# Layer 0's second feed-forward shift and scale: from 32-column TensorE matmuls to VectorE reductions

## The chip, the cores and the metric

The kernel runs on one core of one Trainium2 chip. The metric is the device time of one execution in microseconds (us), the median over several runs; smaller is better. The core has five engines, each with its own in-order instruction stream: TensorE (PE in the profile, with its weight loads as PEld), VectorE (DVE), ScalarE (ACT), GpSimd (POOL) and SyncE (SP). SP and POOL issue the large transfers from device memory here.

## What is computed

A two-layer backbone over 256 latent tokens and 256 context tokens with 1024 features. Each layer has a SwiGLU feed-forward, a token mixing and a second SwiGLU, each behind an RMSNorm with a shift, a scale and a gate. These come from two condition vectors, one for the latent tokens and one for the context tokens, through one large matrix per layer. Cut to what matters:

```
mod_x = (silu(c) @ w_ada[l] + b_ada[l])[:, None, :]      # w_ada[l]: 1024 x 9216
mod_c = silu(c_ctx) @ w_ada[l] + b_ada[l]
sh1, sc1, g1, shm, scm, gm, sh2, sc2, g2 = split(mod_x, 9)
h = h + 0.5 * g1 * swiglu(modulate(rms_norm(h, norm_ffn1[l]), sh1, sc1), w_gate, w_up, w_down)
...                                                      # token mixing with shm, scm, gm
h = h + 0.5 * g2 * swiglu(modulate(rms_norm(h, norm_ffn2[l]), sh2, sc2), ...)
```

sh2 and sc2, the shift and scale of the second feed-forward, are 2 x 1024 numbers for each kind of token. They are first used after the token mixing.

## The kernel before

Activations lie feature-major: features on the 128 partitions, tokens in the free dimension. A weight tile of 128 x 1024 numbers (512 KB) is loaded by SP into a ring of three buffers ("raw") and split by `wload` (lines 124 to 126) into a high and a low float32r part: ACT copies the high part (L125), DVE subtracts to get the low part (L126). The pairs go into a ring of four buffers ("split"). A product is then three matmuls of 512 columns (`mm3`, lines 130 to 132: high x high, high x low, low x high).

The first feed-forward of layer 0 (`ffn`) is the stage that matters here. Its 22 hidden feature tiles are worked in parts of 6, 6, 6 and 4. A hidden tile `ft` takes 24 matmuls into a gate bank "pg" and 24 into an up bank "pu", two banks of each; ACT applies SiLU (L396), DVE multiplies (L397), ACT and DVE split the result into "G" (L398, L399). The first three hidden tiles are computed in an order written out by hand (`first_tiles`, banks "pf"). After a part, and one hidden tile of the next, the part's down projection runs: 8 output tiles of 18 matmuls each into a bank "pd", of which there are three in turn, and DVE adds each to the residual stream "H", one instruction for each kind of token (L259).

Between hidden tiles `run_jobs` calls a share of a list of jobs, so that by hidden tile 19 all are called. The tile scheduler then settles each engine's order; what follows names it where it counts. The jobs of layer 0 are:

- 32 jobs of `ada_dve` (lines 140 to 147), eight for each of g1, shm, scm and gm. A job loads 512 KB of the transposed matrix, 128 output features on the partitions, by POOL's queue into one of 8 buffers "araw" (L144), and takes two DVE instructions of 1024 elements (L147), one for each kind of token, that multiply by the condition vector "cb" and sum along the row.
- 16 jobs of `ada_pe_jobs` (lines 149 to 176) for sh2 and sc2. A job loads 512 KB of the untransposed matrix into one of the same 8 buffers (L158) and issues two matmuls (L160) with 32 columns of weights "csel" and 512 moving columns into the bank "adaps". At the end ACT copies the bank (L165), PE transposes it in four pieces (L168), DVE reduces those (L172) and adds bias and gain.

The two kinds are interleaved, two of the first for one of the second:

```
jobs += jd[:2] + jp[:1]
```

Of the kernel before, what the change touches and what calls it, by code (L numbers as in the profile page):

```python
# [25 lines left out]
BANKS = {"mm": 3, "s": 2, "t": 2, "o": 1}  # L26
PIECES = 4
NT0 = 6
# the order in which the steps of the first tiles are issued (see first_tiles)
START = (  # L30
# [4 lines left out]
)  # L35
# the order in which the steps of the two token mixings are issued (see mixer)
MIX = (
    (
# [10 lines left out]
    ),  # L49
)  # L50
# engines that scale the three tiles of probabilities (A: ScalarE, V: VectorE)
PN = ("AAV", "AVV")
EPS = 1e-6
NEG = -1e30
# [5 lines left out]
def hybrid_backbone(ctx: ExitStack, tc: tile.TileContext, I, out):  # L60
# [8 lines left out]
    def bank(tag, name):  # L69
        return psum.tile([128, 512], F32, tag=tag, name=name, bufs=BANKS[tag])  # L70
# [9 lines left out]
    stt = nc.vector.scalar_tensor_tensor  # L80
    ts_ = nc.vector.tensor_scalar

    # residual stream, feature-major: [feature, feature tile, token]
    H = up.tile([128, KT, TOK], F32, name="H")

    ident = const("ident", [128, 128], I["ident"], nc.scalar)
# [26 lines left out]
        qg8 = late["qg8"] = cp.tile([128, DEPTH], F32, name="qg8")  # L113
        nc.gpsimd.tensor_scalar(qg8, qkg[:, :, 0], 0.125, None, op0=ALU.mult)

# [1 line left out]
    def raw_load(src, n):  # L117
        raw = wp.tile([128, 1024], F32, tag="raw", name="raw", bufs=3)
        nc.sync.dma_start(raw[:, :n], src)
# [17 lines left out]
            mm3(ps, sp[:, 0, o:o + 128], sp[:, 1, o:o + 128], U[0][:, k0 + k, cols], U[1][:, k0 + k, cols],  # L137
                k == 0, k == nk - 1)

# [1 line left out]
    def ada_dve(l, ft, cb, ntok, pool):  # L141
        raw = pool.tile([128, 1024], F32, tag="araw", name="araw", bufs=ABUFS)
        with tc.issue_after(marks["pool"]):
# [1 line left out]
        scr = pool.tile([128, 1024], F32, tag="ascr", name="ascr", bufs=1)  # L145
        for t in range(ntok):
            stt(scr, raw, 1.0, cb[:, t, :], op0=ALU.mult, op1=ALU.mult, accum_out=ada[l][:, ft, t:t + 1])  # L147

    def ada_pe_jobs(src, l, ft0, nchunk, csel, pool, mods):
        box = {}  # L150

        def piece(c, j):
            if not box:
                box["ps"] = bank("o", "adaps")
            ps = box["ps"]
            raw = pool.tile([128, 1024], F32, tag="araw", name="araw", bufs=ABUFS)
            with tc.issue_after(marks["pool"]):
                nc.gpsimd.dma_start(raw, src[:, (c * 4 + j) * 1024:(c * 4 + j + 1) * 1024])  # L158
            for s in range(2):
                mm(ps[32 * j:32 * j + 32, :], csel[:, 2 * j + s, c, :], raw[:, s * 512:(s + 1) * 512],  # L160
                   start=(c == 0 and s == 0), stop=(c == nchunk - 1 and s == 1))

        def end():
            sb = pool.tile([128, 512], F32, tag="adasb2", name="adasb2", bufs=1)
            act(sb, box["ps"], AF.Copy)  # L165
            pt = bank("o", "adapt")
            for b in range(4):
                nc.tensor.transpose(pt[:, b * 128:(b + 1) * 128], sb[:, b * 128:(b + 1) * 128], ident)  # L168
            v = pt.rearrange("p (b j r) -> p b r j", b=4, j=4)
            for c in range(nchunk):  # L170
                f = ft0 + 4 * c
                nc.vector.tensor_reduce(ada[l][:, f:f + 4, :], v[:, :, 2 * c:2 * c + 2, :], axis=AX.X, op=ALU.add)  # L172
            for m in mods:
                ada_fin(l, m)

        return [lambda c=c, j=j: piece(c, j) for c in range(nchunk) for j in range(4)] + [end]

    def ada_fin(l, m, ntok=2, ds=slice(0, KT)):
        i = MODS.index(m)
# [16 lines left out]
        i = MODS.index(m)  # L196
        return ada[l][:, i * KT:(i + 1) * KT, :]

# [1 line left out]
    accs, adds = {}, {}  # L200

    def norm_sq(half, d, eng=nc.gpsimd, pool=None):
        # the sum of squares: tiles 0 .. 6 into one accumulator, tile 7 on its own
        cols = (LAT, CT)[half]
        if d == 0:
            t = npl.tile([128, 256], F32, tag="acc", name="acc", bufs=2)
            accs[half] = [t, None]
        else:
            if pool:
                t = pool.tile([128, 2, TOK], F32R, tag="G", name="sq0", bufs=10)[:, 0, :256].bitcast(F32)  # L210
            else:
                t = npl.tile([128, 256], F32, tag="sq", name="sq", bufs=2)
        act(t, H[:, d, cols], AF.Square)
        if d == KT - 1:
            accs[half][1] = t
        prev = adds.pop(half, None)
        if prev is not None:
            (nc.vector if d >= DV else eng).tensor_tensor(accs[half][0], accs[half][0], prev, ALU.add)
        if 0 < d < KT - 1:
            adds[half] = t  # L220
# [63 lines left out]
        return after  # L284

    def first_tiles(pool, csel, U, src):
        # adaLN's first shift and scale come in feature pieces; NT0 output tiles take each piece as it arrives
        # r, s: 1 / rms of a half of the tokens; a, b, c: a piece of the vectors; w, x: a tile's weights in two parts;
        # u, v: the two parts of a normalised feature tile; m: a feature tile's share of an output tile
        pss, sps, rb, ada_ps, ada_pt, rstd, tmp = [], [], [], {}, {}, {}, {}  # L290

        def r(h):
# [6 lines left out]
            next(rstd[h], None)  # L299

        def a(p, i):
            # a quarter of the rows of w_ada for shift (c = 0) or scale (c = 1), by four column groups of the array
            if i == 0:
                ada_ps[p] = bank("mm", "adaps")
            c, b = divmod(i, 2)
            raw = pool.tile([128, 4, 256], F32, tag="araw", name="araw", bufs=ABUFS)
            nc.sync.dma_start(raw, I["w_ada0"][:, p, c, b])
            for j in range(4):
                mm(ada_ps[p][32 * j:32 * j + 32, :256], csel[:, 2 * j + b, c, :], raw[:, j, :], start=(i == 0),
                   stop=(i == 3))  # L310
# [60 lines left out]
                steps[o[0]](*map(int, o[1:]))  # L371
        return pss

# [1 line left out]
    def ffn(l, w, halves, pool, U, jobs, after, start=None):  # L375
        both = len(halves) == 2
        N = 256 * len(halves)
# [96 lines left out]
                down(p0, n, True)  # L474
            p0 += n

# [1 line left out]
    def mixer(l, pool, U):  # L478
        ctxq = l < DEPTH - 1
        QN = TOK if ctxq else SEQ  # L480
# [84 lines left out]
            return res  # L565

        Q, K = {}, {}
        # feature tiles of w_in: qA 0-2, qB 3-4, qC 5-7, kA 8, kB 9, kC 10-12
        kind = lambda i: "A" if i < 3 or i == 8 else "B" if i < 5 or i == 9 else "C"

        def run(g):
# [165 lines left out]
            act(half[own, qcols], po[oth, qcols], AF.Copy)  # L737
            tt(Y[g // 2][own, qcols], po[own, qcols], half[own, qcols], ALU.add)

        # first projections: latent tokens, then context tokens  # L740
        sk, sq_ = qk_chunk(8), qk_chunk(0)
        sv = vab_load()
        pk, pq = bank("mm", "pk"), bank("mm", "pq")
# [74 lines left out]

                finish(halves, piece, gate, after)

# [1 line left out]
    def load_cb(pool):  # L822
        if "cb" in late and late["cb"][0] is pool:
            return late["cb"][1]
# [8 lines left out]
    def ada_jobs(l, mods, pool, ntok=2):  # L833
        jobs = []
        for m in mods:
            i = MODS.index(m)
            for d in range(KT):
                def job(ft=i * KT + d, m=m, fin=(d == KT - 1)):
                    ada_dve(l, ft, load_cb(pool), ntok, pool)
                    if fin:  # L840
                        ada_fin(l, m, ntok)
                jobs.append(job)
        return jobs

    for l in range(DEPTH):
        last = l == DEPTH - 1
        with tc.tile_pool(name=f"ffn1_{l}", bufs=1) as pool:
            start = None
            if l == 0:
                csel = pool.tile([128, KT, 4, 32], F32, name="csel")  # L850
                nc.gpsimd.memset(csel, 0.0)
                c2 = pool.tile([128, KT, 2], F32, name="c2")
                nc.sync.dma_start(c2, I["ccol"])
                for h in range(2):
                    for i in range(2):
                        w = slice(4 * i, 4 * i + 4)
                        nc.sync.dma_start(H[:, w, (LAT, CT)[h]], I["xT"][:, w, (LAT, CT)[h]])
                for i in range(4):
                    act(csel[:, :, i, 2 * i:2 * i + 2], c2, AF.Silu)
                for h in range(2):  # L860
                    for d in range(KT):
                        norm_sq(h, d, nc.vector, pool)
                U = new_u()

                def start(chunk):
                    return first_tiles(pool, csel, U, chunk)
            if l == 0:
                jd = ada_jobs(0, ("g1", "shm", "scm", "gm"), pool)
                jp = ada_pe_jobs(I["w_ada1"], 0, 48, 4, csel, pool, ("sh2", "sc2"))
                jobs = [late_consts]  # L870
                while jd or jp:
                    jobs += jd[:2] + jp[:1]
                    jd, jp = jd[2:], jp[1:]
            else:
                jobs = ada_jobs(1, ("shm", "scm"), pool) + ada_jobs(1, ("gm", "sh2", "sc2", "g2"), pool, 1)
            Um = []
            ffn(l, 1, (0, 1), pool, U, jobs, next_u(l, 1, Um), start)
            U = Um
# [25 lines left out]


def _tiles(w):
    # [L, K, N] -> [L, 128, N/128, K/128, 128], every output tile contiguous per partition
    L, K, N = w.shape
    return w.reshape(L, K // 128, 128, N // 128, 128).transpose(0, 2, 3, 1, 4).reshape(L, 128, -1)


def _layout(x, c, ctx, c_ctx, w_ada, b_ada, norm_ffn1, w_ffn1_gate, w_ffn1_up, w_ffn1_down, norm_mix, w_in,
# [6 lines left out]
    a["crow"] = np.stack([c[0], c_ctx])  # L919
    a["ccol"] = np.stack([c[0].reshape(KT, 128).T, c_ctx.reshape(KT, 128).T], 2)  # L920
    a["w_ada0"] = w_ada[0, :, :2048].reshape(4, 2, 128, 2, PIECES, 256).transpose(2, 4, 3, 1, 0, 5)
    a["w_ada1"] = w_ada[0, :, 6144:8192].reshape(KT, 128, 4, 512).transpose(1, 2, 0, 3).reshape(128, -1)
    a["w_adaT"] = w_ada.transpose(0, 2, 1).reshape(L, 72, 128, D).transpose(0, 2, 1, 3).reshape(L, 128, -1)
    a["b_ada"] = b_ada.reshape(L, 72, 128).transpose(2, 0, 1)
    g = [v for l in range(L) for v in (norm_ffn1[l], norm_mix[l], norm_ffn2[l])] + [norm_final]
# [54 lines left out]
```

## Time and profile before

| | us |
|---|---|
| median of 3 runs | 1780.79 |
| lowest and highest of the 3 | 1779.76, 1780.89 |
| profiled execution: span from the first to the last instruction | 1777.6 |
| median of the runs less that span | 3.2 |
| PE busy in the span | 1737.7 (98%) |
| DVE busy | 1147.8 (65%) |
| ACT busy | 718.6 (40%) |
| POOL busy | 166.3 (9%) |

The profile is of one execution. It has no time of its own outside the span, so the last but one of the times, 3.2 us, is what lies around the span when it is set beside the median of the runs. A busy PE in it is not a PE at its peak, since the ends of matmuls are modelled: how fast the matmuls follow one another is read from their starts.

### The profile page before, as it was taken

What the parts mean: (1) busy time and instruction counts of PE and PEld (TensorE: products, weight loads), DVE (VectorE), ACT (ScalarE), POOL (GpSimd) and SP (SyncE); (2) the same over time, 40 slices, a digit from 0 to 9 for tenths busy, and PEclk for the clock granted to TensorE, in tenths of its full rate; (3) what the DMA queues carried; (4) which work ended last, traced back from release to release, by engine and by line L of the source; (5) the groups of instructions that cost most, each with busy time, mean ns of one, the idle gap of its engine ahead of it and who ended that gap; (6) DMA issues with size and microseconds to landing.
All of it is one profiled execution on the core that took longest, in us unless ns stands there. A gap on an engine that the chain in (4) does not pass through costs nothing.

```text
span 1777.6 us, 24815 instructions
## 1 busy us (share of the span) xinstructions
PE 1737.7 (98%) x9640; PEld 1476.9 (83%) x9640; DVE 1147.8 (65%) x1971; ACT 718.6 (40%) x1207; POOL 166.3 (9%) x251
## 2 busy tenths in 40 slices
PE   7999999999999999999999999999999999989998
PEld 4777777789898789888888898888888888889997
DVE  5888542336788978994434389954333787976555
ACT  4322222224778944222222252222222477854443
POOL 0311000002000111100000021200000210210000
PEclk9999999999999999999999999999999999999999
DMA  8977432232213237763323267943333233356663
GB/s 323 347 237 224 140 98 80 74 109 83 83 48 104 63 95 255 231 192 86 113 83 107 83 231 248 352 131 103 94 96 103 87 96 95 95 157 189 179 178 117
DMA packets 76693, 258.37 MB, mean 145 GB/s; under 512 B 8944, under 2 KB 11248, under 8 KB 76192
## 3 DMA queue, kind: packets, MB, share of 16 engines
q1 hardware_dynamic: 54096, 176.72, 32.5%
q0 software_dynamic: 21760, 79.38, 13.8%
q8 instruction: 76, 1.25, 0.3%
q10 hardware_dynamic: 720, 0.69, 0.1%
q14 instruction: 41, 0.34, 0.1%
HBM read 250.47 MB, written 1.05 MB: 141 GB/s over the span
## 4 chain that ended last, share of the span: by engine, by line
PE 89%; DVE 3%; ACT 3%; issue 2%; POOL 1%; DMA 1%; SPq 0%; POOLq 0%; DVEq 0%; ACTq 0%
PE pd L132 9%; PE pd L131 9%; PE pd L130 9%; PE pg L130 8%; PE pu L131 8%; PE pu L132 8%; PE pu L130 8%; PE pg L132 8%; PE pg L131 8%; PE adaps L160 2%; PE pq L132 1%; PE pq L130 1%; PE pq L131 1%; PE pt L704 1%; DVE split L126 1%
## 5 line engine op out<-in xcount | busy, mean ns | idle before, releaser
L125 ACT ACTIVATE split<-raw 128x1024 fp32r<-128x1024 f32 (+1 forms) x336 | 332.7, 991 | 564.1 <-PE pd L132 232.1
L126 DVE TENSOR_TENSOR split<-raw,split 128x1024 fp32r<-128x1024 f32 (+1 forms) x336 | 383.8, 1142 | 258.1 <-ACT split L125 255.1
L132 PE MATMUL pd<-G,split 128*128 128x512 f32 (+1 forms) x800 | 273.8, 343 | 0.0
L131 PE MATMUL pd<-G,split 128*128 128x512 f32 (+1 forms) x800 | 273.7, 343 | 0.0
L130 PE MATMUL pd<-G,split 128*128 128x512 f32 (+1 forms) x800 | 273.1, 343 | 0.0
L130 PE MATMUL pg<-Uh,split 128*128 128x512 f32 (+1 forms) x712 | 253.7, 357 | 2.1 <-ACT Uh L250 2.1
L131 PE MATMUL pg<-Ul,split 128*128 128x512 f32 (+1 forms) x712 | 252.0, 354 | 0.1
L132 PE MATMUL pg<-Uh,split 128*128 128x512 f32 (+1 forms) x712 | 252.0, 354 | 0.0
L130 PE MATMUL pu<-Uh,split 128*128 128x512 f32 (+1 forms) x712 | 251.9, 354 | 0.0
L131 PE MATMUL pu<-Ul,split 128*128 128x512 f32 (+1 forms) x712 | 251.8, 354 | 0.0
L132 PE MATMUL pu<-Uh,split 128*128 128x512 f32 (+1 forms) x712 | 251.7, 353 | 0.0
L147 DVE SCALAR_TENSOR_TENSOR ascr<-araw,cb 128x1024 f32<-128x1024 f32 x192 | 234.7, 1222 | 25.3 <-DMA araw<-in_w_adaT 21.4
L259 DVE SCALAR_TENSOR_TENSOR H<-pd,ada,H 128x256 f32<-128x256 f32 x272 | 123.4, 480 | 130.4 <-PE pd L132 130.2
L130 PEld LDWEIGHTS pd<-G,split 128*128 128x128 f32 x800 | 149.7, 188 | 22.6 <-ACT split L125 1.7
L131 PEld LDWEIGHTS pd<-G,split 128*128 128x128 f32 x800 | 150.2, 188 | 20.4
L132 PEld LDWEIGHTS pd<-G,split 128*128 128x128 f32 x800 | 150.0, 188 | 19.5
L130 PEld LDWEIGHTS pg<-Uh,split 128*128 128x128 f32 x712 | 134.9, 190 | 31.1 <-ACT G L398 5.9
L396 ACT ACTIVATE sil<-pg 128x512 f32<-128x512 f32 (+1 forms) x85 | 46.2, 543 | 264.5 <-PE pg L132 264.3
L132 PEld LDWEIGHTS pg<-Uh,split 128*128 128x128 f32 x712 | 134.9, 189 | 18.8
L130 PEld LDWEIGHTS pu<-Uh,split 128*128 128x128 f32 x712 | 135.1, 190 | 18.5
L131 PEld LDWEIGHTS pu<-Ul,split 128*128 128x128 f32 x712 | 134.9, 190 | 18.4
L131 PEld LDWEIGHTS pg<-Ul,split 128*128 128x128 f32 x712 | 134.8, 190 | 18.5 <-DVE Ul L251 0.3
(206 smaller groups left out, 2534.5 us busy)
## 6 DMA issues: line engine op xcount, KB each, us to landing
araw<-in_w_adaT POOLq DMA_DIRECT2D x112, 512.0 KB, 5.1
raw<-in_w_ffn_gate SPq DMA_DIRECT2D x88, 512.0 KB, 4.2
raw<-in_w_ffn_up SPq DMA_DIRECT2D x88, 512.0 KB, 4.1
raw<-in_w_ffn_down SPq DMA_DIRECT2D x96, 384.0 KB, 3.2
raw<-in_w_in SPq DMA_DIRECT2D x26, 512.0 KB, 3.6
araw<-in_w_ada SPq DMA_DIRECT2D x16, 512.0 KB, 10.2
araw<-in_w_ada POOLq DMA_DIRECT2D x16, 512.0 KB, 4.8
raw<-in_w_ffn_down SPq DMA_DIRECT2D x16, 512.0 KB, 3.7
```

Of the source, the lines that this page charges most:

```text
L125: act(sp[:, 0, :n], raw[:, :n], AF.Copy)
L126: tt(sp[:, 1, :n], raw[:, :n], sp[:, 0, :n].bitcast(F32), ALU.subtract)
L130: mm(ps, wh, xh, start=first, stop=False)
L131: mm(ps, wh, xl, start=False, stop=False)
L132: mm(ps, wl, xh, start=False, stop=last)
L147: stt(scr, raw, 1.0, cb[:, t, :], op0=ALU.mult, op1=ALU.mult, accum_out=ada[l][:, ft, t:t + 1])
L160: mm(ps[32 * j:32 * j + 32, :], csel[:, 2 * j + s, c, :], raw[:, s * 512:(s + 1) * 512], start=(c == 0 and s == 0), stop=(c == nchunk - 1 ...
L259: stt(H[:, d, cols], ps[:, off:off + 256], gate[:, d, half:half + 1], H[:, d, cols], op0=ALU.mult, op1=ALU.add)
L396: act(sil[:, cols], pg[:, cols], AF.Silu)
L704: nc.tensor.transpose(pt[:, k * 128:(k + 1) * 128], P[t][:, k * 128:(k + 1) * 128], ident)
```

## The change

The jobs for sh2 and sc2 become 16 more jobs of `ada_dve`. `ada_pe_jobs` goes away, and so does the layout of its copy of the matrix. The list of jobs is then `late_consts` and 48 jobs of one kind, in the order g1, shm, scm, gm, sh2, sc2. The diff, without lines of comment:

```
-    def ada_pe_jobs(src, l, ft0, nchunk, csel, pool, mods):
-        box = {}
-
-        def piece(c, j):
-            if not box:
-                box["ps"] = bank("o", "adaps")
-            ps = box["ps"]
-            raw = pool.tile([128, 1024], F32, tag="araw", name="araw", bufs=ABUFS)
-            with tc.issue_after(marks["pool"]):
-                nc.gpsimd.dma_start(raw, src[:, (c * 4 + j) * 1024:(c * 4 + j + 1) * 1024])
-            for s in range(2):
-                mm(ps[32 * j:32 * j + 32, :], csel[:, 2 * j + s, c, :], raw[:, s * 512:(s + 1) * 512],
-                   start=(c == 0 and s == 0), stop=(c == nchunk - 1 and s == 1))
-
-        def end():
-            sb = pool.tile([128, 512], F32, tag="adasb2", name="adasb2", bufs=1)
-            act(sb, box["ps"], AF.Copy)
-            pt = bank("o", "adapt")
-            for b in range(4):
-                nc.tensor.transpose(pt[:, b * 128:(b + 1) * 128], sb[:, b * 128:(b + 1) * 128], ident)
-            v = pt.rearrange("p (b j r) -> p b r j", b=4, j=4)
-            for c in range(nchunk):
-                f = ft0 + 4 * c
-                nc.vector.tensor_reduce(ada[l][:, f:f + 4, :], v[:, :, 2 * c:2 * c + 2, :], axis=AX.X, op=ALU.add)
-            for m in mods:
-                ada_fin(l, m)
-
-        return [lambda c=c, j=j: piece(c, j) for c in range(nchunk) for j in range(4)] + [end]
...
-                jd = ada_jobs(0, ("g1", "shm", "scm", "gm"), pool)
-                jp = ada_pe_jobs(I["w_ada1"], 0, 48, 4, csel, pool, ("sh2", "sc2"))
-                jobs = [late_consts]
-                while jd or jp:
-                    jobs += jd[:2] + jp[:1]
-                    jd, jp = jd[2:], jp[1:]
+                jobs = [late_consts] + ada_jobs(0, ("g1", "shm", "scm", "gm", "sh2", "sc2"), pool)
...
-    a["w_ada1"] = w_ada[0, :, 6144:8192].reshape(KT, 128, 4, 512).transpose(1, 2, 0, 3).reshape(128, -1)
```

The instructions of the changed kernel have lower line numbers, by 29 below the removed function and by 35 at the end. How the order moves is shown at two places.

PE, where the gate product of hidden tile 4 follows the up product of hidden tile 3 (pu and pg are the two banks). Before:

```order
L130 MATMUL pu<-Uh,split 128x512
L131 MATMUL pu<-Ul,split 128x512
L132 MATMUL pu<-Uh,split 128x512
L160 MATMUL adaps<-araw,csel 32x512 x2
L130 MATMUL pg<-Uh,split 128x512
L131 MATMUL pg<-Ul,split 128x512
L132 MATMUL pg<-Uh,split 128x512
```

With the change:

```order
L130 MATMUL pu<-Uh,split 128x512
L131 MATMUL pu<-Ul,split 128x512
L132 MATMUL pu<-Uh,split 128x512
L130 MATMUL pg<-Uh,split 128x512
L131 MATMUL pg<-Ul,split 128x512
L132 MATMUL pg<-Uh,split 128x512
```

The pair of 32-column matmuls is gone. PE's stream held 15 such places in this feed-forward (the first with two pairs), and at the end four transposes; all the rest of it stands in the same order.

DVE, just ahead of the first additions to the residual stream H in the first down projection. Before:

```order
L147 SCALAR_TENSOR_TENSOR ascr,ada_81<-araw,cb 128x1024 x5
L126 TENSOR_TENSOR split<-raw,split 128x768
L187 TENSOR_TENSOR ada_81<-ada_81,badd 128x16
L147 SCALAR_TENSOR_TENSOR ascr,ada_81<-araw,cb 128x1024 x3
L397 TENSOR_TENSOR sil<-sil,pu 128x512
L126 TENSOR_TENSOR split<-raw,split 128x768
L399 TENSOR_TENSOR G<-sil,G 128x512
L147 SCALAR_TENSOR_TENSOR ascr,ada_81<-araw,cb 128x1024
L259 SCALAR_TENSOR_TENSOR H<-pd,ada_81,H 128x256 x2
L126 TENSOR_TENSOR split<-raw,split 128x768
L147 SCALAR_TENSOR_TENSOR ascr,ada_81<-araw,cb 128x1024 x2
L259 SCALAR_TENSOR_TENSOR H<-pd,ada_81,H 128x256 x2
```

With the change:

```order
L147 SCALAR_TENSOR_TENSOR ascr,ada_81<-araw,cb 128x1024 x3
L368 TENSOR_TENSOR sil<-sil,pu 128x512
L158 TENSOR_TENSOR ada_81<-ada_81,badd 128x16
L147 SCALAR_TENSOR_TENSOR ascr,ada_81<-araw,cb 128x1024
L370 TENSOR_TENSOR G<-sil,G 128x512
L147 SCALAR_TENSOR_TENSOR ascr,ada_81<-araw,cb 128x1024
L126 TENSOR_TENSOR split<-raw,split 128x768
L147 SCALAR_TENSOR_TENSOR ascr,ada_81<-araw,cb 128x1024
L230 SCALAR_TENSOR_TENSOR H<-pd,ada_81,H 128x256
L147 SCALAR_TENSOR_TENSOR ascr,ada_81<-araw,cb 128x1024
L230 SCALAR_TENSOR_TENSOR H<-pd,ada_81,H 128x256
L126 TENSOR_TENSOR split<-raw,split 128x768
```

From the first L147 of the program on, 36 instructions L147 and 11 splits stand ahead of the first pair of additions before. With the change 36 and 11 stand ahead of the second addition of that pair, the last L147 between the two.

The 60 instructions L147 left after the first down projection's first tile are spread as far as the additions of the sixth output tile of the second down projection, two for each output tile; before, the 28 left all stood ahead of that projection. From there to the end of the program DVE's order is the same, but for the reductions of L172 and the bias and gain of sh2 and sc2, which stood at the start of the third down projection and now stand in the second. POOL issues the same number of 512 KB transfers, 48, now all of one kind; ACT loses L165 alone; SP's order is the same.

## Rows read from the trace of the kernel before

**Rows 1.** Page, part 4: the chain that ended last, by line.

```profile
PE pd L132 9%; PE pd L131 9%; PE pd L130 9%; PE pg L130 8%; PE pu L131 8%; PE pu L132 8%; PE pu L130 8%; PE pg L132 8%; PE pg L131 8%; PE adaps L160 2%; PE pq L132 1%; PE pq L130 1%; PE pq L131 1%; PE pt L704 1%; DVE split L126 1%
```

**Rows 2.** Windows over layer 0's first feed-forward; the first row names the columns.

```profile
core 0: us, PE busy (x) PEld busy (x) DVE busy (x) ACT busy (x) POOL busy (x), PEclk, DMA share, GB/s
...
67.00:100.00 33.00, 33.00 (x136) 23.06 (x135) 32.10 (x51) 6.99 (x9) 6.96 (x13) 1.00 0.83 298
...
220.00:260.00 40.00, 40.00 (x169) 31.02 (x168) 14.75 (x22) 8.21 (x10) 0.00 (x0) 1.00 0.32 87
260.00:300.00 40.00, 40.00 (x167) 30.07 (x166) 12.91 (x15) 9.92 (x12) 0.00 (x0) 1.00 0.32 91
...
sum 289.00, PE 289.00 PEld 215.73 DVE 171.38 ACT 71.50 POOL 24.27; mean PE 36.12 PEld 26.97 DVE 21.42 ACT 8.94 POOL 3.03
```

**Rows 3.** Timeline of PE: start us, us, engine, line, operation, count.

```profile
66.94 0.40 PE L366 MATMUL pf<-Ul,split 128*128 128x512 f32 x1
67.26 1.92 PE L160 MATMUL adaps<-araw,csel 128*32 128x512 f32 x8
...
69.44 0.39 PE L131 MATMUL pg<-Ul,split 128*128 128x512 f32 x1
...
80.22 1.90 PE L160 MATMUL adaps<-araw,csel 128*32 128x512 f32 x4
...
93.19 1.90 PE L160 MATMUL adaps<-araw,csel 128*32 128x512 f32 x4
...
178.60 0.39 PE L130 MATMUL pg<-Uh,split 128*128 128x512 f32 x1
...
189.25 0.39 PE L132 MATMUL pu<-Uh,split 128*128 128x512 f32 x1
...
341.20 0.40 PE L130 MATMUL pd<-G,split 128*128 128x512 f32 x1
...
342.11 0.40 PE L132 MATMUL pd<-G,split 128*128 128x512 f32 x1
```

**Rows 4.** Tile adaps: duration ns min/median/max, first and last start us.

```profile
L160 PE MATMUL adaps<-araw,csel x64: 592/592/617, 67.3 to 339.2; 128*32 128x512 f32 x64
```

**Rows 5.** Groups of DVE, 53 to 342 us: count, busy us, mean ns, idle before.

```profile
L147 DVE SCALAR_TENSOR_TENSOR ascr<-araw,cb 128x1024 f32<-128x1024 f32 x64 | 78.3, 1223 | 19.7 <-DMA araw<-in_w_adaT 18.7
```

**Rows 6.** Timeline of DVE, columns as in rows 3.

```profile
57.04 1.23 DVE L147 SCALAR_TENSOR_TENSOR ascr<-araw,cb 128x1024 f32<-128x1024 f32 x1 [2.87 <-DMA araw<-in_w_adaT]
...
90.64 1.22 DVE L147 SCALAR_TENSOR_TENSOR ascr<-araw,cb 128x1024 f32<-128x1024 f32 x1
...
91.90 1.23 DVE L147 SCALAR_TENSOR_TENSOR ascr<-araw,cb 128x1024 f32<-128x1024 f32 x1
...
123.10 0.08 DVE L147 DVE_READ_ACCUMULATOR ascr<-araw,cb 128x1 f32 x1
125.50 0.88 DVE L259 SCALAR_TENSOR_TENSOR H<-pd,ada,H 128x256 f32<-128x256 f32 x2 [2.31 <-PE pd L132]
...
129.71 0.87 DVE L259 SCALAR_TENSOR_TENSOR H<-pd,ada,H 128x256 f32<-128x256 f32 x2
```

**Rows 7.** Window of DVE from the first L147 to the first addition's wait.

```profile
57.04:123.19 66.15, 63.20 (x100) 1.00 0.84 298
```

**Rows 8.** Waits of DVE in 53 to 342 us: us in total, times, longest.

```profile
DVE split L126 <- ACT split L125: 54.7, 27, 6.5
...
DVE ascr L147 <- DMA araw<-in_w_adaT: 18.7, 7, 4.1
```

**Rows 9.** Transfers issued in 53 to 210 us: count, KB each, median us to landing.

```profile
araw<-in_w_adaT POOLq DMA_DIRECT2D x30, 512.0 KB, 4.7
araw<-in_w_ada POOLq DMA_DIRECT2D x16, 512.0 KB, 4.8
```

## Prediction, made before the changed kernel was run

> **What bounds the kernel now.** I read the chain that ended last first [rows 1]: nearly all of its long lines are PE's, and one of them is the work that the change removes, the 32-column matmuls of L160 with 2% of the span, some 36 us at that rounding. The windows over layer 0's first feed-forward [rows 2] say the same of the stage where those matmuls stand: PE is busy in all of its 289.00 us at a granted clock of 1.00, which is 2.4 GHz, the clock's upper level. So there each microsecond taken from PE's stream comes off the end, if nothing new makes PE wait. The same rows show who could do that: DVE is busy 32.10 of 33 us from 67 to 100 us, and 14.75 of 40 from 220 to 260. The change takes work from the full engine and gives work to one that is nearly full early and half empty late.
>
> **What it removes from PE.** The timeline of PE [rows 3] gives the price by starts, since busy times of matmuls overlap. From one burst of L160 (80.22) to the next (93.19) are 12.97 us: a burst, 24 matmuls into pg and 24 into pu. Hidden tile 9, which has no burst, begins at 178.60 and its last matmul starts at 189.25; with one step more of (189.25 - 178.60) / 47 = 0.227 it takes 10.88. A burst thus costs 12.97 - 10.88 = 2.09 us. The first burst has two jobs: from 66.94 to 69.44 are 2.50 us, where two ordinary steps would be 0.46, so 2.04. The tile's view [rows 4] counts 64 recorded L160; 8 are in the first burst and 4 in each other, so there are 1 + 56 / 4 = 15 bursts. They cost 15 x 2.04 = 30.6 to 15 x 2.09 = 31.4 us. At the end the four transposes stand between the starts 341.20 and 342.11, 0.91 where two steps are 0.47: 0.44 us. Removed: 31.0 to 31.8; I take 31.5, nearer to the upper end, as 14 of the 15 bursts are of the second kind.
>
> That first burst also settles a question of price. It has 8 records in 1.92 us, each other has 4 in 1.90 [rows 3]: the two jobs of the first lie on different 32-column strips and ran beside each other, while a burst with one job leaves three strips empty and runs its four records one after another. The Trainium skill (TensorEngine Tiling (Array Packing), sections Theoretical Speedup and Key Properties) states that products with 32 columns can run up to four times as fast because strips work in parallel, and that a change of tiling mode drains the engine. The step into the first burst, 66.94 to 67.26, is 0.32 where an ordinary one is 0.23 [rows 3], which agrees with a drain. By the four-fold rule the removed work would be worth only about 8 us; the bursts of one strip each do not have that speed, and the sum stays by the rows.
>
> **What it adds to DVE.** Sixteen jobs of two L147 each are 32 instructions. One is 1223 ns [rows 5], and two in a row start 1.26 us apart (90.64, 91.90) [rows 6]: 32 x 1.26 = 40.3 us. In the stage DVE has 171.38 of 289.00 us [rows 2]; after, about 211.7 of 289.00 - 31.5 = 257.5. In sum it fits, with 46 us over. ACT's copy L165 and DVE's four reductions go; the chain has neither, so I cost them at nothing.
>
> **Where it is tight.** DVE is in order, and its list is now packed from the first L147 to the second down projection. The place that ends first is the first down projection: three pd banks are in use, so PE can't begin output tile 3 before DVE has added tile 0 to H. Before the change DVE was ready at 123.18, the end of the last L147 ahead, and then waited 2.31 us for PE (addition at 125.50) [rows 6]. With the change the same number of L147 and splits, 36 and 11, lie ahead of the second addition. DVE had 66.15 us from the first L147 to there and was busy in 63.20 [rows 7]; the 2.95 idle were mostly waits for PE's releases through ACT, which come earlier now. So DVE finishes tile 0, its two additions taking 0.88, between 123.18 - 2.95 + 0.88 = 121.1 and 123.18 + 0.88 = 124.1. PE has lost five bursts by then: tile 0 is ready at 125.50 - 5 x 2.09 = 115.05, and tile 3 is due two tiles later. A tile takes 129.71 - 125.50 = 4.21 [rows 6], so that is 123.5. The margin is +2.4 to -0.6 us: a wait of 0 to 0.6, and I take 0, since the first end has its reason in the trace and the second assumes that waits for PE stay where PE comes earlier. In the next tiles DVE has no L147 with tile 1 and two with each of the others, some 4.2 us of work for 4.2 us of PE, so the lateness stays about what it is and can't pile up fast.
>
> Later, 60 L147 (60 x 1.26 = 75.6 us) lie between there and the sixth tile of the second down projection. PE needs for that 7 x 4.21 + 6 x 10.88 + 6 x 4.21 = 120 us. DVE's other work in it is what it does from 220 to 300 us before, where it has no jobs and PE does the same two things: 14.75 + 12.91 = 27.7 of 80 us [rows 2]. For 120 us that is 41.5, and some 2 us more because PE has no bursts in it. Together 117 to 119 of 120: level with PE, with little over.
>
> **Transfers.** 46 loads for the jobs were issued from 53 to 210 us [rows 9], 16 of them for PE's jobs, at the same 512 KB and landing time (4.7, 4.8) as the others. The number stays, and a buffer is now always freed by DVE. Before, DVE waited 18.7 us in 7 times for such loads [rows 8] while PE's jobs held buffers till their burst; this goes. I cost the loads at nothing: one is wanted per 2.5 us at the fastest, and the eight buffers cover 8 x 2.5 = 20 us against 4.7.
>
> **The sum.** 0 to +0.6 of waits against -31.0 to -31.8: -30.4 to -31.8, and -31.5 is likeliest. The profiled span of 1777.6 becomes 1746.1; with the same 3.2 us around it the median of 1780.79 becomes **1749.3 us**.
>
> **Rivals.**
> *DVE's lateness reaches PE.* For it: the margin of 2.4 to -0.6 us, and a stretch with 1 to 3 us to spare in 120. DVE's rows come from a trace in which it was less packed; 5% more on 96 L147 is 6 us. Against: in 67 to 100 us it was 97% busy and PE didn't wait. The price is a job of two L147 (2.5 us) at one to three places, pd banks first: 1749.3 + 2.5 to 7.5 = 1751.8 to 1756.8.
>
> *DVE's queue becomes the bound, and the kernel is slower.* The mechanism: an L147 that waits for its load holds the splits behind it on DVE, and PE waits for those. The waits of DVE on loads had a mean of 18.7 / 7 = 2.7 us [rows 8]. If each of the 48 jobs had one, 128 us would meet the 46 that DVE has over; PE would be held 82 us, and the time would be 1749.3 + 82 = 1831. It decides against the change from (46 + 31.5) / 48 = 1.6 us of wait per job. Against it: those 7 waits came with buffers held by PE's jobs, which go.
>
> *The gain is given back.* PE arrives 31.5 us earlier at the second half of the stage and at the mixing, and waits there for something that does not move with it: about 1780. Against it: the moved vectors are done in the second down projection, and DVE's waits there are for PE and ACT [rows 8].
>
> *The removed matmuls are worth a quarter.* If a burst of one strip holds up the matmuls behind it by a fourth of its length, as it would if the other strips went on, 31.4 / 4 = 8 us go: 1773. The starts before and after a burst speak against it [rows 3]. This is what the four-fold rule of the page named above would make of it.
>
> **How the numbers follow.** My forecast has 0.76, lateness that reaches PE 0.18, the slower queue 0.02, the gain given back 0.02, a quarter's worth 0.02. The range of 8 in 10 is 1747.5 to 1755.5: below, the larger removal and the scatter of the runs; above, most of the first rival. 0.2% of this kernel, 3.6 us, is about what a measurement of it can tell from no change. Faster by more than that: forecast, first rival and the quarter, 0.96; within it 0.02; slower 0.02.
>
> **What would show it.** In the profile of the changed kernel no L160 and no L168 of before; hidden tiles that begin 10.88 us apart wherever no down projection lies between; PE busy in all of the stage, and the stages behind it as long as before; 32 more L147, the last of them in the second down projection; DVE's waits for loads nearly gone. At output tile 3 of the first down projection, PE waiting for H would be the first rival. Wrong it would be if PE's waits for DVE in this stage summed to over 5 us, or if the hidden tiles took longer than 10.88.

## The result, and the profile after

| | us |
|---|---|
| changed kernel, median of 4 runs (lowest, highest) | 1749.51 (1749.39, 1751.63) |
| kernel before, on the same chip, median of 4 runs | 1780.84 (1779.76, 1780.96) |
| ratio, 95% interval | 0.9825, 0.9811 to 0.9839 |
| span of the profiled execution, before and after | 1777.6, 1747.2 |

The change takes 31.3 us off the median, 1.75%. The forecast was 31.5 off and 1749.3.

The windows of the changed kernel, to set beside [rows 2] (columns as there; the last row is the stage up to the third down projection):

```profile
67.00:100.00 33.00, 33.00 (x147) 27.25 (x147) 32.76 (x52) 8.45 (x11) 4.84 (x9) 1.00 0.78 254
220.00:260.00 40.00, 40.00 (x175) 32.50 (x174) 25.75 (x41) 9.07 (x10) 0.00 (x0) 1.00 0.42 118
260.00:300.00 40.00, 40.00 (x178) 33.14 (x177) 13.71 (x15) 12.08 (x16) 0.00 (x0) 1.00 0.27 80
53.00:311.00 258.00, 258.00 (x1129) 211.64 (x1128) 205.23 (x323) 71.61 (x90) 24.66 (x46) 1.00 0.61 192
```

PE is still busy in all of the stage at a granted clock of 1.00. DVE, the third of the engine columns, has 205.23 of 258 us where it had 171.38 of 289. The work it took over now reaches into the stretch from 220 to 260 us (25.75 in place of 14.75); from 260 to 300, where no job is left, it is busy 13.71 us, beside 12.91 before.

PE's timeline after, beside [rows 3]: the first matmul of hidden tiles 3 to 6, of the first down projection, and of its output tile 3:

```profile
67.53 0.40 PE L130 MATMUL pg<-Uh,split 128*128 128x512 f32 x1
...
78.45 0.39 PE L130 MATMUL pg<-Uh,split 128*128 128x512 f32 x1
...
89.33 0.39 PE L130 MATMUL pg<-Uh,split 128*128 128x512 f32 x1
...
100.21 0.39 PE L130 MATMUL pg<-Uh,split 128*128 128x512 f32 x1
...
111.09 0.40 PE L130 MATMUL pd<-G,split 128*128 128x512 f32 x1
...
123.70 0.39 PE L130 MATMUL pd<-G,split 128*128 128x512 f32 x1
```

From 78.45 on the tiles begin 10.88 us apart, where a tile with a burst took 12.97 [rows 3]. No row of this view says that PE waited, and the waits of PE have no entry between 53 and 380 us.

DVE, its group of L147 from 53 to 311 us (beside [rows 5]), then its timeline at the tight place (beside [rows 6]) and at the end of the jobs, then its waits from 53 to 311 us (beside [rows 8]):

```profile
L147 DVE SCALAR_TENSOR_TENSOR ascr<-araw,cb 128x1024 f32<-128x1024 f32 x96 | 117.1, 1220 | 4.2 <-DMA araw<-in_w_adaT 2.9
```

```profile
118.98 0.48 DVE L230 SCALAR_TENSOR_TENSOR H<-pd,ada,H 128x256 f32<-128x256 f32 x1
119.38 1.21 DVE L147 SCALAR_TENSOR_TENSOR ascr<-araw,cb 128x1024 f32<-128x1024 f32 x1
...
120.52 0.48 DVE L230 SCALAR_TENSOR_TENSOR H<-pd,ada,H 128x256 f32<-128x256 f32 x1
120.92 0.95 DVE L126 TENSOR_TENSOR split<-raw,split 128x768 fp32r<-128x768 f32 x1
...
234.74 1.23 DVE L147 SCALAR_TENSOR_TENSOR ascr<-araw,cb 128x1024 f32<-128x1024 f32 x1
```

```profile
DVE split L126 <- ACT split L125: 32.0, 16, 4.7
DVE sil L368 <- PE pu L132: 16.3, 6, 3.1
DVE H L230 <- PE pd L132: 3.3, 2, 1.9
DVE ascr L147 <- DMA araw<-in_w_adaT: 2.9, 1, 2.9
```

DVE is through with output tile 0 at 121.00 (120.52 + 0.48), and PE comes to output tile 3, which takes over that bank, at 123.70: DVE is 2.7 us ahead. This distance, from the end of what DVE owes to the moment at which PE wants it, is called the margin below. Its waits for loads have gone from 18.7 us in 7 times to 2.9 in one. The last of the 96 L147 ends in the second down projection.

### The profile page after: what moved, and what is told of

It reads as the page before. It is cut to its first block, busy times and chain, and to the rows that moved or that the text cites. A ratio compares the mean times of both kernels' runs of the same rounds, so it can differ in the third digit from the quotient of the medians.

```text
span 1747.2 us, 24756 instructions
## 1 busy us (share of the span) xinstructions
PE 1707.2 (98%) x9572; PEld 1473.6 (84%) x9572; DVE 1180.4 (68%) x2031; ACT 718.0 (41%) x1206; POOL 167.3 (10%) x251
## 4 chain that ended last, share of the span: by engine, by line
PE 89%; ACT 3%; DVE 3%; issue 2%; POOL 1%; DMA 1%; SPq 0%; POOLq 0%; DVEq 0%; ACTq 0%
PE pd L131 9%; PE pd L132 9%; PE pd L130 9%; PE pu L130 8%; PE pu L131 8%; PE pu L132 8%; PE pg L130 8%; PE pg L132 8%; PE pg L131 8%; PE pq L130 1%; PE pq L132 1%; PE pq L131 1%; PE pt L675 1%; PE pv L576 1%; PE pv L578 1%
## 5 line engine op out<-in xcount | busy, mean ns | idle before, releaser
L147 DVE SCALAR_TENSOR_TENSOR ascr<-araw,cb 128x1024 f32<-128x1024 f32 x224 | 273.2, 1220 | 9.9 <-DMA araw<-in_w_adaT 5.7
L132 PEld LDWEIGHTS pg<-Uh,split 128*128 128x128 f32 x712 | 134.9, 189 | 18.7
L130 PEld LDWEIGHTS pu<-Uh,split 128*128 128x128 f32 x712 | 135.1, 190 | 18.4
L131 PEld LDWEIGHTS pg<-Ul,split 128*128 128x128 f32 x712 | 134.8, 190 | 18.7 <-DVE Ul L222 0.3
L132 PEld LDWEIGHTS pu<-Uh,split 128*128 128x128 f32 x712 | 134.9, 190 | 18.4
```

Of the source, the lines that this page charges most:

```text
L130: mm(ps, wh, xh, start=first, stop=False)
L131: mm(ps, wh, xl, start=False, stop=False)
L132: mm(ps, wl, xh, start=False, stop=last)
```

## Experiments

Ten kernels, each timed in three rounds beside the kernel before. All of them start from the changed kernel, but for four_strips, which starts from the kernel before.

| kernel | median us (lowest to highest) | ratio to before, 95% | against the changed kernel, us |
|---|---|---|---|
| `neither` | 1748.53 (1747.54 to 1750.98) | 0.9816, 0.9799 to 0.9832 | -1.0 |
| bursts_back | 1780.64 (1778.57 to 1781.67) | 0.9999, 0.9989 to 1.0008 | +31.1 |
| four_strips | 1757.63 (1756.81 to 1758.76) | 0.9869, 0.9854 to 0.9884 | +8.1 |
| extra48 | 1757.37 (1756.73 to 1760.91) | 0.9871, 0.9857 to 0.9886 | +7.9 |
| extra24 | 1753.55 (1752.57 to 1754.63) | 0.9848, 0.9833 to 0.9863 | +4.0 |
| late24 | 1749.84 (1749.63 to 1749.90) | 0.9823, 0.9808 to 0.9837 | +0.3 |
| early4 | 1750.79 (1750.36 to 1752.23) | 0.9827, 0.9811 to 0.9844 | +1.3 |
| extra96 | 1774.72 (1772.15 to 1776.25) | 0.9967, 0.9955 to 0.9978 | +25.2 |
| two_buffers | 1766.27 (1765.84 to 1766.72) | 0.9920, 0.9903 to 0.9937 | +16.8 |
| one_buffer | 1777.10 (1772.61 to 1779.90) | 0.9979, 0.9968 to 0.9990 | +27.6 |

The last column is a difference of medians of runs made at different times; the medians of before beside them lie between 1780.79 and 1781.0 (late24 and early4 ran on another chip than the other eight, with 1781.0 there). A difference of 1 us is no more than the scatter, the spread of runs of one kernel. Line numbers in the rows below move by a few where a kernel has lines more.

### What the work costs on each engine: `neither`, bursts_back

`neither` drops the jobs of sh2 and sc2 from the changed kernel and holds those two vectors constant.

```
-                jobs = [late_consts] + ada_jobs(0, ("g1", "shm", "scm", "gm", "sh2", "sc2"), pool)
+                jobs = [late_consts] + ada_jobs(0, ("g1", "shm", "scm", "gm"), pool)
```

> The changed kernel without the 16 jobs for layer 0's sh2 and sc2 (they stay at a constant, so neither PE's bursts nor the 32 L147 are there). Theory, that the gain is PE's removed time alone and that DVE's new work costs nothing: 1749.5 us, within 1 us of the changed kernel. Rival, that DVE's fuller queue costs PE something: faster than the changed kernel by what it costs, 1 to 7 us.

Measured 1748.53: within the scatter of the changed kernel's time. DVE without the 32 instructions L147 (reductions, in what follows) is busy in 169.09 of the 258 us from 53 to 311, 36 us less, and the time is the same within that scatter. What DVE took over is hidden.

`bursts_back` is the changed kernel with 15 bursts of 32-column matmuls between the jobs again, on data that is there anyway; nothing reads their sums.

```
+        if l == 0 and 16 <= ft < 64 and ft % 3 == 0 and "csel" in late:
...
+            for s in range(2):
+                mm(late["burst"][32 * j:32 * j + 32, :], late["csel"][:, 2 * j + s, c, :], raw[:, s * 512:(s + 1) * 512],
+                   start=(c == 0 and s == 0), stop=(c == 3 and s == 1))
```

> The changed kernel, with PE's 15 bursts of 32-column matmuls put back at nearly the old places, on data that is loaded anyway and with a result that nothing reads; no transposes, no load more, DVE's 48 jobs stay. Theory, PE's time by itself: 15 x 2.04 to 2.09 = 30.6 to 31.4 us more than the changed kernel, 1780.1 to 1780.9. Rival, that the gain came from the loads or from DVE waiting less for them: it stays near 1749.5 to 1755 us.

Measured 1780.64, the time of before: +31.1 us, 2.07 for each of the 15 bursts. DVE has all its 96 reductions here too. So the gain is PE's time for the bursts; a part from the order, the loads or DVE's waits is no larger than the scatter of about 1 us.

### Is a burst's price that of its matmuls? four_strips

The kernel before, its 16 TensorE jobs put together in four bursts of four jobs, each job on another 32-column strip (the 32 of the 128 output partitions that its matmuls write, `32 * j` to `32 * j + 32` in the code).

```
+            for s in range(2):
+                for j in range(4):
+                    mm(box["ps"][32 * j:32 * j + 32, :], csel[:, 2 * j + s, c, :], raws[j][:, s * 512:(s + 1) * 512],
...
-                    jobs += jd[:2] + jp[:1]
+                    jobs += jd[:8] + jp[:1]
```

> The kernel before, with the 16 jobs on PE issued four at a time, one for each 32-column strip, in 4 bursts. By the price of a burst in the trace (2.09 us whether one strip or two are in it) 4 x 2.1 + 0.44 = 8.8 us of PE remain: 1749.5 + 8.8 = 1758.3 us. Rival, that a job costs its 2 us wherever it stands: 16 x 2.0 = 32, so about 1781 us.

Measured 1757.63, 8.1 us above the changed kernel; four bursts of 2.09 and the transposes' 0.44 make 8.8. PE's timeline around one of its bursts:

```profile
89.03 0.39 PE L132 MATMUL pu<-Uh,split 128*128 128x512 f32 x1
89.35 1.92 PE L187 MATMUL adaps<-araw,csel 128*32 128x512 f32 x16
91.21 0.50 PE L130 MATMUL pg<-Uh,split 128*128 128x512 f32 x1
```

The profile has two records for each of these matmuls, so a job is four. Sixteen records on four strips take 1.92 us, as long as four did on one strip (1.90 in [rows 3]). That bears out the four-fold rule of the Trainium skill (TensorEngine Tiling (Array Packing), section Theoretical Speedup), for strips that are issued side by side. The same 32 matmuls of sh2 and sc2 cost 31 us as fifteen bursts and 8 as four. So a burst costs about 2 us with one, two or four strips filled; a burst with more than one job on a strip was not run. The changed kernel is still faster, since DVE does the work for nothing.

### How much more could DVE take? extra48, extra24, late24, early4, extra96

All five have further instructions like L147, whose sums nothing reads. They differ in which jobs get them.

```
+        if l == 0 and 16 <= ft < 64 and ft % 1 == 0:
+            stt(scr, raw, 1.0, cb[:, 0, :], op0=ALU.mult, op1=ALU.mult, accum_out=xacc[:, ft:ft + 1])
```

That is extra48. In extra24 the condition ends with `ft % 2 == 0`, in late24 it is `40 <= ft < 64`, in early4 `16 <= ft < 20`; extra96 adds two to each job.

> The changed kernel with a third L147 in each of the 48 jobs (its sum is not used): 48 x 1.26 = 60.5 us more of DVE in the first feed-forward. In the stage up to the third down projection DVE has 258 - 205 = 53 us left, and pd's three banks give 8.4 us of grace. Theory, that DVE's work is free as long as it fits: 1749.5 to 1752 us. Rival, that DVE is already the bound from the first L147 to the second down projection: up to 60 us more, and at least 10.

Measured +7.9 us, between the two: both intervals missed. The waits of PE from 53 to 380 us (us in total, times, longest):

```profile
PE pg L133 <- DVE split L127: 1.9, 1, 1.9
PE pd L133 <- DVE split L127: 1.8, 2, 1.2
PE pd L131 <- DVE H L233: 1.3, 1, 1.3
```

These 5.0 us lie between 128 and 154 us: three in the first down projection, one just behind. All the rest of the stage, where most of the 60 us stand, has none. So the question became whether the amount of work counts or its place in DVE's order.

> The changed kernel with a third reduction in every second job, whose sum nothing reads: 24 more instructions of DVE of 1.26 us, 30.2 us. Up to the end of the first down projection only 2 of the 24 come ahead (49 in place of 47 jobs' instructions), 2.5 us against the 2.8 us that DVE was ahead at output tile 3; the others stand where DVE idled. Theory (what DVE adds costs nothing until the first down projection's margin is used up): 1749.5 to 1751, no wait of PE for DVE over 0.5 us in the stage. Rival (each microsecond of DVE costs its share, 7.9 of 60.5 as in the run with 48): 1753.5.

My theory missed: 1753.55, as the rival said. But the rival's reason is not what the trace shows. PE waits twice, both times in the first down projection, and nowhere else in the stage (PE's timeline):

```profile
126.18 0.40 PE L132 MATMUL pd<-G,split 128*128 128x512 f32 x1
128.00 0.49 PE L133 MATMUL pd<-G,split 128*128 128x512 f32 x1 [1.42 <-DVE split L127]
...
132.54 0.39 PE L132 MATMUL pd<-G,split 128*128 128x512 f32 x1
134.25 0.47 PE L131 MATMUL pd<-G,split 128*128 128x512 f32 x1 [1.32 <-DVE H L233]
```

The two steps of 1.82 and 1.71 are 3.1 us longer than two ordinary ones of 0.23; the rest of the 4.0 us is within the scatter and not traced. Only two of the 24 instructions had come ahead of the end of that projection, but DVE's order there had changed too: a split that stood behind the second addition to H (120.92 above) now stands behind the sixth, with six L147 between.

```profile
125.37 0.48 DVE L233 SCALAR_TENSOR_TENSOR H<-pd,ada,H 128x256 f32<-128x256 f32 x1
...
126.99 0.95 DVE L127 TENSOR_TENSOR split<-raw,split 128x768 fp32r<-128x768 f32 x1
```

PE was at the matmul that needs it at 126.41 (126.18 + 0.23). The next kernel keeps the amount and moves the place; the one behind it adds a few instructions, all of them at the front.

> The changed kernel with a third reduction, whose sum nothing reads, in the last 24 of the 48 jobs: as many more instructions of DVE (24, 30.2 us) as in the run that had one in every second job and took 1753.55, but none of them ahead of the end of the first down projection, where DVE's order is that of the changed kernel. Theory (the place decides: only the first down projection has no DVE time over): 1749.5, at most 1751, and no wait of PE for DVE in the stage. Rival (the amount decides): 1753.5.

Measured 1749.84, no wait of PE in the stage, though DVE is busier than in extra24:

```profile
53.00:311.00 258.00, 258.00 (x1129) 211.62 (x1128) 233.54 (x371) 71.53 (x89) 24.22 (x45) 1.00 0.60 192
```

Twenty-four more instructions cost nothing where all stand behind the first down projection, and 4.0 us where two of them stand ahead of its end and the scheduler moves a split back with them: the place decides.

> The same with a third reduction in the first four jobs alone, 4 instructions of DVE, 5.0 us. In the order all of that stands ahead of the fourth addition to H (38 in place of 36 jobs' instructions), six jobs' instructions lie between the first addition and the next split, and that split comes behind the sixth addition, as in the run with one in every second job; in the changed kernel it comes behind the second. Theory (the place decides): PE waits for that split and for an addition at output tiles 2 to 4 of the first down projection, 1 to 4 us, so 1750.5 to 1753.5. Rival (the amount decides, 4 in 24 of the 4.0 us): 1750.2 with no wait of PE.

Measured 1750.79, at the lower end of the theory's interval and 0.6 from the rival's value; this run alone does not part them. The waits of PE of 1 to 4 us that the theory expected are not there: the stage has none in the profile's list. DVE's timeline, then PE's from the start of the projection:

```profile
127.32 0.48 DVE L233 SCALAR_TENSOR_TENSOR H<-pd,ada,H 128x256 f32<-128x256 f32 x1
...
127.72 2.69 DVE L127 TENSOR_TENSOR split<-raw,split 128x768 fp32r<-128x768 f32 x3
```

```profile
111.26 0.40 PE L131 MATMUL pd<-G,split 128*128 128x512 f32 x1
...
128.72 0.50 PE L133 MATMUL pd<-G,split 128*128 128x512 f32 x1
```

The split stands behind the sixth addition here too, though with five reductions between the first addition and it (the expectation says six). It was done 17.35 us after the projection's start (127.72 + 2.69 / 3 - 111.26), and the matmul that needs it began at 17.46, 0.42 after the one before it in place of 0.23. In extra24 that matmul began 18.86 us after the start (128.00 - 109.14). The new order had used up the margin, and little more: PE came 0.19 us late, and the rest of the 1.3 us is within the scatter.

> The changed kernel with two more reductions in each of the 48 jobs, whose sums nothing reads: 96 more instructions of DVE, 121 us, where DVE idles 53 us from 53 to 311 us and 34 from there to 369. Up to the end of the first down projection the order holds as many of them as the run with 48 (54 in place of 47), so 8 us are lost there as in that run; then 43 stand between the second down projection and the third, where PE needs 65 us and DVE has 54 us of them and some 20 of its own, and 34 behind that. Theory (DVE becomes the bound behind the first down projection too): 1770 to 1795, PE waiting for DVE between 220 and 380 us by over 10 us. Rival (only the first down projection's margin counts): 1757.

Measured 1774.72 (+25.2): the theory's interval. With 121 us more, PE waits for DVE behind the first down projection too. The trace has 15.0 us of waits between 53 and 400 us, 6.0 ahead of 220 us and 9.0 behind it, a little under the "over 10" of the theory:

```profile
PE pg L133 <- DVE split L127: 6.0, 2, 3.0
PE pd L133 <- DVE split L127: 6.0, 4, 3.0
PE pd L131 <- DVE H L234: 3.0, 2, 1.7
```

### What if the loads were late? two_buffers, one_buffer

The prediction's second rival was a DVE queue held up by loads. Here the 48 jobs of the changed kernel get one or two buffers of their own in place of eight (with two, the first loads of the program have seven).

```
+        one = l == 0 and 16 <= ft < 64
-        raw = pool.tile([128, 1024], F32, tag="araw", name="araw", bufs=ABUFS)
+        raw = pool.tile([128, 1024], F32, tag="araw1" if one else "araw", name="araw1" if one else "araw", bufs=2 if one else ABUFS)
```

> The changed kernel with the 48 jobs' loads through two buffers of their own in place of eight (and one buffer less for the first loads of the program, for space). A buffer's round is the load, 4.7 us, and the job's two reductions, 2.5, so with two buffers a job can start each 3.6 us at best; DVE took one each 3.4 us up to the first addition (18 jobs in 62 us) and one each 4.8 later. DVE's order stays nearly as it was (34 in place of 36 jobs' instructions ahead of that addition). Theory (the loads are covered by the eight buffers, and a load that is late holds the queue of DVE only where DVE has none over): DVE's waits for loads grow to 5 to 25 us, nearly all ahead of 125 us, and the time is 1749.5 to 1756. Rival (each job then holds DVE's queue by 1.1 us or more, 53 in all, against the 53 us that DVE idles, and PE waits for the splits behind): 1757 to 1770.

Measured 1766.27: the rival's interval. The waits of DVE for loads are 21.8 us, within the theory's 5 to 25, but half of them, 11.1 us, lie behind 125 us, where it had almost none; and PE waits twice (waits of DVE from 53 to 311 us, of PE from 53 to 345):

```profile
DVE ascr L148 <- DMA araw<-in_w_adaT: 21.8, 23, 3.0
```

```profile
PE pd L130 <- DVE H L231: 8.5, 2, 5.5
```

Both times it is output tile 3 of a down projection that waits for the addition of tile 0, the place that the prediction named. The first, in PE's timeline:

```profile
124.42 0.40 PE L132 MATMUL pd<-G,split 128*128 128x512 f32 x1
127.80 0.77 PE L130 MATMUL pd<-G,split 128*128 128x512 f32 x1 [2.98 <-DVE H L231]
128.37 0.63 PE L131 MATMUL pd<-G,split 128*128 128x512 f32 x1
...
131.27 0.39 PE L132 MATMUL pd<-G,split 128*128 128x512 f32 x1
```

DVE had time over as a sum (201.11 busy of 258 us), but each wait for a load pushes back what follows it in DVE's order, and the next down projection finds DVE late. PE's first hidden tile behind the first three begins at 68.49 in place of 67.53, so 1.0 us is lost ahead of it; the first loads have one buffer less there, but that start differs between runs anyway (see the gain kept, below), so the cause is not shown. My theory had taken idle time in the stage for a cushion.

> The same with one buffer for all 48 jobs: a job each 7.2 us at best (4.7 for the load, 2.5 for the reductions), 346 us in all, so to about 400 us, past the end of this feed-forward. DVE's order puts 20 in place of 36 jobs' instructions ahead of the first additions, 28 in place of 47 at the end of that projection and the last of the 96 at the end of the fourth. DVE must wait for each load, 4.7 us or what the order leaves of it. By the prediction's second rival, waits of more than 1.6 us for each job cost more than the change brings: slower than 1780.8. Against it, what stands between two jobs in the new order covers part of each load: 90 jobs' instructions up to 369 us leave DVE 200 us of idle time for 226 us of loads, so that the time would be 1750 to 1785.

Measured 1777.10, inside the second interval, and still faster than before (0.1 to 0.3%). From 53 to 380 us DVE waits 105.0 us for 44 loads, 2.4 us each:

```profile
DVE ascr L148 <- DMA araw<-in_w_adaT: 105.0, 44, 3.8
```

The order settled by the scheduler spreads the jobs as far as the fourth down projection, so part of each load is covered, and PE waits 15.3 us in all from 53 to 400 us. The rest of the 27.6 us is not traced.

## Why the prediction was right

**The removed matmuls: right.** 31.0 to 31.8 were forecast from the starts; bursts_back gives 31.1, and the change 31.3. The step that mattered was to price a burst by the distance of its neighbours' starts (2.09) and not by matmuls; four_strips confirms it with bursts of four jobs at the price of one. The rival of a quarter's worth is out for these bursts, and its number, 8 us, is what four bursts of four strips cost.

**DVE's cost of nothing: right.** The run `neither` puts it at 1.0 us, inside the scatter. In sum DVE has 205.23 of 258 us, where 211.7 of 257.5 was forecast, though a reduction took what it was priced at (1220 ns beside 1223). The later stretch, "117 to 119 of 120", is measured by DVE's window from the end of output tile 0 to the end of the last reduction, 113.69 us busy of 114.97, and PE did not wait in it:

```profile
121.00:235.97 114.97, 113.69 (x186) 1.00 0.67 209
```

**The tight place: right, with the margin at its upper end.** Forecast were +2.4 to -0.6 us at output tile 3 of the first down projection, measured 2.7. The end that I took, that the 2.95 us of idle time go when PE comes earlier, is the one that held (121.00 against 121.1): from the first reduction to there DVE has no wait for ACT, where it had 2.2 us of them before. The place of the splits was luck in part: in extra24, with two more reductions ahead of the end of that projection, the scheduler put one split behind four more additions, and that costs 4.0 us. The first rival, at 0.18, was a real one.

**The loads: right** for eight buffers (one wait, 2.9 us, ahead of the first reduction as before). What two_buffers shows, though, is that the rival's working was wrong. It set the sum of the waits against the 46 us that DVE has over in the stage, so 21.8 us of waits would have cost nothing. In fact these 23 waits of 0.95 us on the mean came with a loss of about 16 us. In the changed kernel 47.9 of the 52.8 us that DVE idles from 53 to 311 us lie behind 235.97, and PE's two waits in two_buffers end at 127.80 and 234.34, ahead of that. The run one_buffer misses the rival's bound of 1.6 us of wait per job from the other side: it has 105 us of waits, 2.2 for each of the 48 jobs, and is not slower than before; its order spreads the jobs further, so that part of each load is covered. The same mistake stood in my expectations of extra48 and two_buffers: a sum over the stage in place of the distance to the next due time. In extra24 I did count up to the due time, but not the split that moved.

**The gain kept: right.** The median fell by as much as PE's time. The two profiled spans differ by 30.4, 0.9 less than the medians, because the profiled execution of before was a quick one: in 13 later runs of that kernel the span has a median of 1779.0 and lies 1.8 to 1.9 below the time. The 3.2 us around the span thus set a quick span beside a median; in the forecast the same number is taken off and put back, so it does no harm. The median spans, 1779.0 and 1747.45, differ by 31.5. The start of PE's first hidden tile behind the first three also differs from run to run, 65.58 in extra24 to 67.70 in early4, with 67.53 in the changed kernel.

No kernel here beats the changed one by more than the scatter. `neither`, which leaves the work out altogether, is a bound for moving it anywhere, and lies 1.0 us below.

## What to carry to other kernels

Price work that stands between another engine's instructions by the starts of its neighbours, and ask how many bursts it makes and how many strips each fills, not how many instructions it has. Before giving work to an engine with idle time, find the next place where the busiest engine needs its result, and count what stands ahead of that place in its queue: 24 instructions cost 4.0 us where two of them, and a split that moved with them, came in ahead of such a place, and 0.3 where all stood behind it. Idle time behind a due time is no cushion for lateness ahead of it.

## What the runs showed of the hardware

A wait of PE can cost more than its length. In two_buffers PE's matmuls behind the wait of 5.49 us follow at 0.43 us in place of 0.23, from 234.34 to 240.43 (PE's timeline):

```profile
234.34 0.77 PE L130 MATMUL pd<-G,split 128*128 128x512 f32 x1 [5.49 <-DVE H L231]
234.91 0.63 PE L131 MATMUL pd<-G,split 128*128 128x512 f32 x1
235.34 0.63 PE L132 MATMUL pd<-G,split 128*128 128x512 f32 x1
...
240.03 0.56 PE L131 MATMUL pd<-G,split 128*128 128x512 f32 x1
240.43 0.40 PE L132 MATMUL pd<-G,split 128*128 128x512 f32 x1
```

The granted clock there is 0.50, the 1.2 GHz level (windows, columns as in [rows 2]: in the wait, behind it, and later):

```profile
228.40:234.30 5.90, 0.45 (x2) 0.02 (x1) 5.87 (x12) 2.39 (x4) 0.54 (x1) 0.94 0.64 169
235.00:239.60 4.60, 4.60 (x12) 3.55 (x11) 4.37 (x9) 0.00 (x0) 0.54 (x1) 0.50 0.77 228
242.00:246.00 4.00, 4.00 (x18) 3.21 (x18) 3.59 (x8) 0.65 (x2) 0.54 (x1) 1.00 0.73 208
```

The 14 steps from 234.34 to 240.43 took 6.09 us, 2.8 more than 14 of 0.23. Behind the wait of 2.98 us the 8 steps from 127.80 to 131.27 took 3.47, 1.6 more. In extra48 steps at 0.43, with a granted clock of 0.50, follow waits of 1.31 and 1.20 us with two matmuls between, and the wait of 1.86; they cost about 3 of its 7.9 us. In extra24 the waits of 1.42 and 1.32 us, 6 us apart, were followed by none. The Trainium skill (TensorE: Matmul & The Clock Gate, section Wait — 56ns, not 53.3ns?) states that back-to-back matmuls of 512 columns start 426.7 ns apart at the lower clock, which agrees with the 0.43. For the upper clock it has 215.7 ns, and the rows here have 0.227 to 0.234 us; for this kernel the rows decide.
